# A layer's mixers written as tasks: waits that sleep, marks for order, wider paces

## The chip, the cores and the metric

The kernel runs on one core of one Trainium2 chip. The metric is the device time of one execution in microseconds; the time before is 1107.42 us, the median of three runs from 1107.02 to 1109.54 us. Profiles come from one further execution each. In the profile PE is TensorE (PEld its weight loads), DVE is VectorE, ACT is ScalarE, POOL is GpSimd and SP is SyncE, which issues most transfers.

## The reference

One decoder layer for 256 tokens of width 2048, in float32. Two mixers read one normalised input through one projection, their outputs go through one output projection, and a SwiGLU feed-forward part follows:

```
n = rms_norm(x, attn_norm_g);  proj = n @ w_in          # 2048 -> 5672 columns
g_qkv = silu(causal_short_conv(g_qkv, conv_w))          # q, k, v of the GLA mixer
gla   = gated linear attention (4 heads) of q, k, v, gate(g_lr), rms_norm, * silu(g_out)
nsa   = softmax attention (8 heads, 2 key heads) over compressed, selected and window keys,
        the three summed with sigmoid gates; keys and queries rms-normed
h     = x + concat(gla, nsa) @ w_out
out   = h + (silu(m @ w_gate) * (m @ w_up)) @ w_down    # m = rms_norm(h), d_ff = 5632
```

With 256 tokens all blocks are selected and the window holds all tokens, so the selected and the window branch are two full causal attentions with keys of their own. The compressed branch has 15 keys, each made by a small network from 32 tokens.

## The kernel before, in words

**Arithmetic.** Each large product is made of three matmuls of float32r parts: `hi` of the tokens with `hi` and `lo` of the weights, and `lo` with `hi`. A weight chunk of 512 rows and 512 columns is loaded on SP's queue into `raw` (3 buffers, `load`, L126), then split: ACT copies `hi` (L137), DVE subtracts to `lo` (L138; 4 buffers of 2 rows of tiles each). `chunk` (L273) makes its 24 matmuls (L283) and yields 2 units after each one; where a projection has two column parts, after each pair. A projection (`proj`, L291) is 4 chunks, 192 units; its end `evac` reads the PSUM banks.

**Mains and side tasks.** The order of the work is that of Python generators. `drive(mains, pace)` (L98) runs projections and, for every `pace` units, calls `side()` once (L83). `side` advances one step of a task: the first of the list `urgent`, or, when that is empty, the first of `later`. A task that has to wait for a result of another engine does so by empty yields, each of which uses one call: `for _ in range(8): yield`. `background` holds row sums for the feed-forward part (`sum_rows`, L1068: two loads, four adds on DVE at L1079, two stores on POOL's queue at L1083), one step for every `rate[0]` units. `drain` (L93) runs what is left of a list without any main beside it. The call order ranks the instructions. From it the framework lists each engine's instructions by when it reckons them ready, so that a later call's instruction can stand ahead of an earlier one's: in the profile Exp of the decay (L545) comes before Silu of conv (L502), which is called earlier. Each engine then takes its list in order.

**The tasks.** The stages run in this order: a first projection (low-rank gate and half of the output gate), GO1 (its other half), qq and kk (queries and keys of GLA, pace 1.5), v0 and v1 (its values, pace 2), KC, KS, KW and NQ0 (compressed, selected and window keys with their values, half of NSA's queries, pace 2.5), NQ1 (the other half, pace 2.5), then the first half of w_out (L973, 8 chunks, 384 units, pace 2), the drains of both lists, and the second half of w_out.

- `conv` (L481, urgent; for qq, kk, v0, v1): scaled tokens from ACT (L478), 8 empty calls, then for each of two pairs two calls of transposes (L210), four taps (ACT L490, DVE L492) and `dst`. For values `to_v` (L507) applies Silu (L510, L511), waits 10 calls and transposes again in two.
- `gla_mix` (L647, later): `gla_decay` (L529) has seven levels, each with Exp on ACT (L545, L547), GAP calls, products on DVE and GAP calls again (GAP0 8 for the first pair of heads, GAP1 4 for the second); `gla_scores` (L570) has ten matmuls (L584) for each of four heads; `gla_out` (L602) reads the values and appends `gla_turn` (L628, urgent, 20 empty calls and 2 of transposes).
- `turn_kc` (8 empty calls and 4), `key_turn` (L725, 15 empty calls, 1 of transposes; four of them), `turn_q` (L848, 18 empty calls and 4; two of them), all urgent.
- `compress` (L751, later): for keys and for values, loads of four weight tiles on POOL's queue (L760), 9 calls, 16 small matmuls (L779), again 9 calls and 16 matmuls, then 6 calls, a transpose and Silu (L794 for keys, L798 for values), 9 calls and a matmul (L803 or L819).
- `nsa_mix` (L950, later): for four tiles, `nsa_scores` (L859, 16 calls: L873 to L876) and `nsa_out` (L908, 15 calls for the first half of the tokens and 25 for the second: transposes and L946).

The tiles of 128 partitions and 1024 elements named `g` come in the large from one ring, `g4`, of 24 buffers: the normalised tokens, keys, values, the compression's weights and the row sums share it.

Of the kernel before, what the change touches and what calls it, by code (L numbers as in the profile page):

```python
# [17 lines left out]
NT = S // P  # L18
# [19 lines left out]
def kernel(  # L38
# [42 lines left out]
    urgent, later, background = [], [], []  # L81

    def side():  # L83

        for queue in (urgent, later):
            while queue:
                try:
                    next(queue[0])
                    return
                except StopIteration:  # L90
                    queue.pop(0)

# [121 lines left out]


    cols = kp.tile([P, 164], F32, name="cols")
    pc = bank()
# [7 lines left out]
    def cols_rest():  # L225
        for _ in range(8):
            yield
        nc.gpsimd.memset(w2b, 0.0)
        with behind(last["dma"]):
            small_loads()  # L230
        for _ in range(20):
            yield
        pc = bank()
        transpose(pc[:, 0:P], rows2)
        transpose(pc[:, P:P + 20], rows[:20, :], 20)
        nc.vector.tensor_copy(cols[:, 36:164], pc[:, 0:P])
        nc.vector.tensor_copy(cols[:, 16:36], pc[:, P:P + 20])
        TS(kgain, gains[:, 1:4], gains[:, 0:1], None, ALU.mult)


# [240 lines left out]
    def conv(u, ct, dst):  # L481

        for _ in range(8):
            yield
        for pair in range(2):
            ps = yield from turn_pair(u, pair)
            y = g2([2, S])
            for c in range(2):
                ch = ct + 2 * pair + c
                act(y[:, c, :], ps[:, c, :], AF.Copy, scale=cw[:, 3, ch:ch + 1])  # L490
                for i in range(1, 4):
                    STT(y[:, c, i:], ps[:, c, :S - i], cw[:, 3 - i, ch:ch + 1], y[:, c, i:], ALU.mult, ALU.add)  # L492
            yield from dst(pair, y)
# [6 lines left out]
    def to_qk(near, far):  # L500
        def f(pair, y):
            act(near[:, pair, 0 if near is kk else 1], y[:, :, 0:P], AF.Silu)  # L502
            act(far[:, pair, 0 if far is qq else 1], y[:, :, S - 1:P - 1:-1], AF.Silu)
            yield
        return f

    def to_v(b):  # L507
        def f(pair, y):
            v = g2([2, S])
            act(v[:, :, 0:P], y[:, :, 0:P], AF.Silu)  # L510
            act(v[:, :, P:], y[:, :, S - 1:P - 1:-1], AF.Silu)  # L511
            c0 = (4 * b + 2 * pair) * P
            for _ in range(10):
                yield
            p = bank()
            for t in range(NT):
                for c in range(2):
                    transpose(p[:, t * S + c * P:t * S + (c + 1) * P], v[:, c, t * P:(t + 1) * P])
                yield
            for t in range(NT):  # L520
                nc.scalar.copy(v_sb[t][:, c0:c0 + 2 * P], p[:, t * S:(t + 1) * S])
            v_ready.add(2 * b + pair)
        return f

    m_h, m_l = {}, {}
    v_ready = set()
    GAP0, GAP1 = 8, 4

# [99 lines left out]
    def gla_turn(h, y):  # L628
        for _ in range(20):
            yield  # L630
        if h % 2 == 0:
            m_h[h // 2], m_l[h // 2] = g4([4, S], F32R), g4([4, S], F32R)
        p = bank()
        for j in range(2):
            for t in range(NT):
                transpose(p[:, j * S + t * P:j * S + (t + 1) * P], y[:, t, j * P:(j + 1) * P])
            yield
        put_mix(h // 2, slice(2 * (h % 2), 2 * (h % 2) + 2), slice(0, S), p.rearrange("p (j s) -> p j s", j=2))

    def in_parts(hi, lo, ps):  # L640
# [6 lines left out]
    def gla_mix():  # L647
        res = [{} for _ in range(4)]
        yield from gla_decay(0, GAP0)
        for _ in range(6):  # L650
# [27 lines left out]
    def turn_kc(u):  # L678
        for _ in range(8):
            yield  # L680
        st["uT"] = g4([2, 2, S])
# [43 lines left out]
    def key_turn(br, t, kk):  # L725
        for _ in range(15):
            yield
        p = bank()
# [5 lines left out]
        act(kh, pv, AF.Copy, scale=g)  # L734
        STT(kl, pv, g, f32(kh), ALU.mult, ALU.subtract)

    kcm = cp.tile([P, 2 * NCMP], F32, name="kcm")
# [13 lines left out]
    def compress():  # L751
# [13 lines left out]
        for w in range(2):  # L765
# [20 lines left out]
            nc.vector.tensor_copy(hs, ph[:, :P])  # L786
            for _ in range(6):
                yield
# [6 lines left out]
            else:  # L795
                hid3 = g2([2, P])
                nc.gpsimd.memset(hid3, 0.0)
                act(groups(hid3), thrice(hid[:, :N2].rearrange("p (h n) -> p h n", h=2)), AF.Silu)  # L798
            for _ in range(9):
                yield  # L800
# [47 lines left out]
    def turn_q(kv, q):  # L848
        for _ in range(18):
            yield  # L850
        qf, qh, ql = g4([4, S]), g4([4, S], F32R), g4([4, S], F32R)
# [98 lines left out]
    def nsa_mix():  # L950
# [3 lines left out]
        def ready(u):  # L954
            while u[0] not in nq:
                yield
# [15 lines left out]

    def w_out_half(half):  # L973
        for n in range(4):
            banks = [bank() for _ in range(NT)]
# [299 lines left out]
    def down_last():  # L1275
# [68 lines left out]
        for t, bk in enumerate((banks[4], at[1])):  # L1344
# [11 lines left out]
    drive([proj(1024, ev_conv(8, to_v(0))), proj(1536, ev_conv(12, to_v(1)))], 2)  # L1356
    rate[0] = 18
    drive([proj(C_KC, ev_kc), proj(C_KS, ev_kv(0)),
           proj(C_KW, ev_kv(1), ((0, 256), (256, 280))), proj(C_NQ, ev_nq(0))], 2.5)
    later.append(nsa_mix())  # L1360
    drive([proj(C_NQ + 512, ev_nq(1))], 2.5)
    rate[0] = 14
    drive([w_out_half(0)], 2)
    drain(urgent)
    drain(later)
# [44 lines left out]
```

## Time and profile before

| | us |
|---|---|
| median of 3 runs | 1107.42 |
| lowest, highest | 1107.02, 1109.54 |
| the profiled execution | 1108.26 |
| its span, first to last instruction | 1106.5 |
| PE busy | 1096.7 |
| DVE busy | 992.7 |
| ACT busy | 751.5 |
| POOL busy | 71.7 |

The span is 1.76 us less than the profiled execution's own time; what lies around it is in every run. The first matmul of kk is at 80.79 us, that of KC at 157.09, that of w_out's first half at 291.44 and that of its second half at 369.46; the feed-forward part begins at 416.91 us. In a row of the waits the columns are the sum, the number and the longest; in the timeline, start, length, engine, line, operation, written tile and read tiles, shape, count, and in brackets the idle time before and what ended it.

### The profile page before, as it was taken

Reading aid. Unit: us, or ns where it says so; the run is one execution under the profiler, and the core shown is the slowest. Engines: PE = TensorE matmul, PEld = TensorE weight load, DVE = VectorE, ACT = ScalarE, POOL = GpSimd, SP = SyncE. Lnnn points to the kernel's source line nnn. Section 1 sums busy time; section 2 is a strip of 40 time slices with the busy share of each in tenths; the row PEclk is TensorE's granted clock in tenths of the full one; section 3 lists DMA queues with packets and bytes.
Section 4 is the critical chain, followed back from the end, with each engine's and each line's share of the span. In section 5 each row is a group of like instructions: output and inputs, shape, how many; then the busy total and the mean of one; then the engine's idle time right before and its main releaser. Section 6 shows DMA issues by size and latency. Waiting matters only on the chain.

```text
span 1106.5 us, 14596 instructions
## 1 busy us (share of the span) xinstructions
PE 1096.7 (99%) x5290; PEld 900.4 (81%) x5290; DVE 992.7 (90%) x1277; ACT 751.5 (68%) x1017; POOL 71.7 (6%) x134
## 2 busy tenths in 40 slices
PE   9999999999999999999999999999999999999998
PEld 8888788897777787888888788888888888888886
DVE  6678887879689788997999999999999999999997
ACT  6646867554566596667586776768586866768684
POOL 4110000123200000000000000000000000000000
PEclk9999999999999999999999999999999999999999
DMA  7999677579765646785565657566665657577763
GB/s 271 340 332 346 210 256 243 196 274 375 282 239 192 236 154 218 242 307 200 192 219 202 217 185 256 195 234 215 216 227 201 214 198 252 182 252 234 237 229 114
DMA packets 124850, 259.61 MB, mean 235 GB/s; under 512 B 6709, under 2 KB 8793, under 8 KB 124778
## 3 DMA queue, kind: packets, MB, share of 16 engines
q1 hardware_dynamic: 113514, 219.86, 58.1%
q0 software_dynamic: 10368, 37.75, 9.2%
q10 hardware_dynamic: 896, 1.07, 0.3%
q8 instruction: 41, 0.67, 0.3%
q14 instruction: 31, 0.25, 0.1%
HBM read 239.78 MB, written 18.87 MB: 234 GB/s over the span
## 4 chain that ended last, share of the span: by engine, by line
PE 88%; DVE 5%; DMA 3%; ACT 3%; issue 1%; POOL 0%; ACTq 0%; DVEq 0%
PE bank L283 44%; PE bank L1147 36%; PE bank L210 3%; DMA raw<-in_w_in_dram 2%; PE bank L1288 2%; DVE ftwo L642 2%; DVE lo L138 1%; PE bank L584 1%; PE bank L946 1%; PE bank L873 1%; ACT hi L137 1%; DMA fraw<-in_w_down_dram 1%; ACT ftwo L641 0%; PE bank L779 0%; DVE g L1178 0%
## 5 line engine op out<-in xcount | busy, mean ns | idle before, releaser
L1147 PE MATMUL bank<-ftwo,g 128*128 128x512 f32 x1848 | 431.6, 392 | 0.2 <-ACT ftwo L641 0.2
L1147 PEld LDWEIGHTS bank<-ftwo,g 128*128 128x128 f32 x1848 | 342.4, 188 | 76.6 <-DVE ftwo L642 3.3
L283 PE MATMUL bank<-hi,g 128*128 128x512 f32 (+1 forms) x1088 | 321.5, 375 | 0.3 <-ACT hi L137 0.2
L642 DVE TENSOR_TENSOR ftwo<-fraw,ftwo 128x1536 fp32r<-128x1536 f32 (+1 forms) x130 | 257.9, 1984 | 8.8 <-ACT ftwo L641 7.5
L641 ACT ACTIVATE ftwo<-fraw 128x1536 fp32r<-128x1536 f32 (+1 forms) x130 | 216.9, 1670 | 32.9 <-DMA fraw<-in_w_up_dram 23.2
L283 PE MATMUL bank<-ftwo,g 128*128 128x512 f32 x960 | 221.4, 391 | 0.4 <-ACT bank L1259 0.4
L283 PEld LDWEIGHTS bank<-hi,g 128*128 128x128 f32 x1088 | 192.4, 188 | 31.7 <-issue 0.8
L283 PEld LDWEIGHTS bank<-ftwo,g 128*128 128x128 f32 x960 | 179.2, 188 | 39.9 <-ACT bank L1259 2.6
L137 ACT ACTIVATE hi<-raw 128x1024 fp32r<-128x1024 f32 (+3 forms) x124 | 130.6, 1057 | 95.8 <-PE bank L283 73.2
L283 PE MATMUL bank<-lo,g 128*128 128x512 f32 (+3 forms) x544 | 193.6, 375 | 0.9 <-DVE lo L138 0.6
L138 DVE TENSOR_TENSOR lo<-raw,hi 128x1024 fp32r<-128x1024 f32 (+3 forms) x124 | 150.0, 1216 | 34.3 <-ACT hi L137 33.6
L641 ACT ACTIVATE ftwo<-g 128x1024 fp32r<-128x1024 f32 x74 | 78.2, 1057 | 69.4 <-DVE g L1178 41.1
L283 PEld LDWEIGHTS bank<-lo,g 128*128 128x128 f32 x544 | 98.4, 188 | 16.1 <-DVE lo L138 1.0
L642 DVE TENSOR_TENSOR ftwo<-g,ftwo 128x1024 fp32r<-128x1024 f32 x74 | 90.3, 1220 | 10.5 <-ACT ftwo L641 10.5
L642 DVE TENSOR_TENSOR ftwo<-fsum,ftwo 128x1024 fp32r<-128x1024 f32 x74 | 90.2, 1219 | 0.0
L641 ACT ACTIVATE ftwo<-fsum 128x1024 fp32r<-128x1024 f32 x74 | 77.5, 1048 | 6.4 <-DVE fsum L1180 5.1
L1271 ACT COPY g<-bank 128x512 f32<-128x512 f32 x80 | 45.9, 589 | 39.4 <-PE bank L283 37.6
L1178 DVE TENSOR_TENSOR g<-fraw 128x1024 f32<-128x1024 f32 x56 | 67.5, 1219 | 0.0
L1259 ACT COPY bank<-g 128x512 f32<-128x512 f32 x80 | 45.2, 593 | 14.3 <-DVE f L1208 13.0
L641 ACT ACTIVATE g<-bank 128x512 fp32r<-128x512 f32 x46 | 27.3, 599 | 33.0 <-PE bank L210 27.4
L210 PE MATMUL bank<-ident,g 128*128 128x128 f32 (+3 forms) x230 | 42.5, 277 | 1.5 <-ACT g L1043 0.7
L1136 POOL DMA_DIRECT2D g<-sums x16 | 8.5, 531 | 511.5 <-DVE ftwo L642 482.8
(247 smaller groups left out, 908.3 us busy)
## 6 DMA issues: line engine op xcount, KB each, us to landing
fraw<-in_w_gate_dram SPq DMA_DIRECT2D x86, 512.0 KB, 4.0
fraw<-in_w_down_dram SPq DMA_DIRECT2D x42, 1024.0 KB, 5.1
raw<-in_w_in_dram SPq DMA_DIRECT2D x36, 1024.0 KB, 6.5
fraw<-in_w_up_dram SPq DMA_DIRECT2D x70, 512.0 KB, 4.8
sums<-g POOLq DMA_DIRECT2D x32, 512.0 KB, 5.0
raw<-in_w_out_dram SPq DMA_DIRECT2D x16, 1024.0 KB, 5.8
g<-in_w_gate_dram SPq DMA_DIRECT2D x16, 512.0 KB, 7.4
g<-in_w_up_dram SPq DMA_DIRECT2D x16, 512.0 KB, 8.1
```

What stands on the lines that cost most here:

```text
L137: act(h[:, i:i + n], r[:, k + i:k + i + n], AF.Copy)
L138: last["d"] = TT(o[:, i:i + n], r[:, k + i:k + i + n], f32(h[:, i:i + n]), ALU.subtract)
L210: return nc.tensor.transpose(o, i, ident[:n, :n])
L283: last["mm"] = mm(bk[t], a[:, k, t * P:(t + 1) * P], m[:, off:off + w], start=(first_ and k == 0 and i == 0), stop=(end and k == 3 and i = ...
L584: mm(p[:, j * P:(j + 1) * P], u, w, start=True, stop=True)
L641: act(hi, ps, AF.Copy)
L642: last["d"] = TT(lo, ps, f32(hi), ALU.subtract)
L1147: mm(banks[q], x, m, start=todo[q] == total[q], stop=todo[q] == 1)
L1178: TT(s1, r[:, 1:3], r[:, 3:4].to_broadcast([P, 2, 512]), ALU.add)
L1259: nc.scalar.copy(banks[qs[n][t]], h_sb[n][:, t, :])
L1271: nc.scalar.copy(h_sb[n][:, t, :], bs[t])
L1288: mm(bk, u, m, start=(first and i == 0), stop=(end and i == 2), skip_group_check=onto)
```

## The change

`side` gets a table of sleeping tasks. A task may yield a number; it is then passed over for so many calls, and the call goes to the next task of `urgent` that is awake, or else to the first of `later`. At each call the numbers of all urgent tasks go down by one. The empty yields of conv, to_v, gla_turn, turn_kc, key_turn and turn_q become such numbers, longer than before. The set `done` holds marks: gla_mix waits for the marks of all four pairs of q and k, nsa_mix for those of the four key_turns, and two assertions stand in conv and in w_out. Two waits of the compression grow from 6 to 10 and from 9 to 14 calls, GAP1 from 4 to 6. The paces grow from 2.5 to 2.8 (KC to NQ0), from 2.5 to 2.7 (NQ1) and from 2 to 2.6 (first half of w_out), and the background rate goes from 18 to 16 units from KC on, until the first half of w_out.

```diff
+    asleep = {}
+
     def side():
 
+        for task in urgent:
+            asleep[task] = max(asleep.get(task, 0) - 1, 0)
         for queue in (urgent, later):
-            while queue:
+            while True:
+                task = next((t for t in (urgent if queue is urgent else later[:1]) if not asleep.get(t)), None)
+                if task is None:
+                    break
                 try:
-                    next(queue[0])
+                    asleep[task] = next(task) or 0
                     return
                 except StopIteration:
-                    queue.pop(0)
+                    queue.remove(task)
...
     def conv(u, ct, dst):
 
-        for _ in range(8):
-            yield
+        assert "cols" in done
+        yield 14
...
             act(far[:, pair, 0 if far is qq else 1], y[:, :, S - 1:P - 1:-1], AF.Silu)
+            done.add((near is kk, pair))
             yield
...
             c0 = (4 * b + 2 * pair) * P
-            for _ in range(10):
-                yield
+            yield 16
             p = bank()
...
-    GAP0, GAP1 = 8, 4
+    GAP0, GAP1 = 8, 6
...
     def gla_turn(h, y):
-        for _ in range(20):
-            yield
+        yield 22
...
     def gla_mix():
         res = [{} for _ in range(4)]
+        while not all((i, pair) in done for i in (False, True) for pair in range(2)):
+            yield
         yield from gla_decay(0, GAP0)
...
     def turn_kc(u):
-        for _ in range(8):
-            yield
+        yield 12
...
     def key_turn(br, t, kk):
-        for _ in range(15):
-            yield
+        yield 18
...
         STT(kl, pv, g, f32(kh), ALU.mult, ALU.subtract)
+        done.add(("key", br, t))
...
             nc.vector.tensor_copy(hs, ph[:, :P])
-            for _ in range(6):
+            for _ in range(10):
                 yield
...
-            for _ in range(9):
+            for _ in range(14):
                 yield
             pk = bank()
...
     def turn_q(kv, q):
-        for _ in range(18):
-            yield
+        yield 20
...
         def ready(u):
-            while u[0] not in nq:
+            while u[0] not in nq or not all(("key", br, t) in done for br in range(2) for t in range(NT)):
                 yield
...
     def w_out_half(half):
+        assert all(("out", h) in done for h in range(4))
...
-    rate[0] = 18
+    rate[0] = 16
     drive([proj(C_KC, ev_kc), proj(C_KS, ev_kv(0)),
-           proj(C_KW, ev_kv(1), ((0, 256), (256, 280))), proj(C_NQ, ev_nq(0))], 2.5)
+           proj(C_KW, ev_kv(1), ((0, 256), (256, 280))), proj(C_NQ, ev_nq(0))], 2.8)
     later.append(nsa_mix())
-    drive([proj(C_NQ + 512, ev_nq(1))], 2.5)
+    drive([proj(C_NQ + 512, ev_nq(1))], 2.7)
     rate[0] = 14
-    drive([w_out_half(0)], 2)
+    drive([w_out_half(0)], 2.6)
```

More of the change, by code (lines that the diff above doesn't have):

```diff
@@ L213, in rsqrt_ @@
         nc.gpsimd.tensor_tensor(o, i, mhalf[:i.shape[0], :i.shape[1]], ALU.pow)
+    done = set()
     cols = kp.tile([P, 164], F32, name="cols")
@@ L238, in cols_rest @@
         TS(kgain, gains[:, 1:4], gains[:, 0:1], None, ALU.mult)
+        done.add("cols")
     def flip(src, q, gcol, hi, lo, pairs=range(2), between=None):
@@ L638, in gla_turn @@
         put_mix(h // 2, slice(2 * (h % 2), 2 * (h % 2) + 2), slice(0, S), p.rearrange("p (j s) -> p j s", j=2))
+        done.add(("out", h))
     def in_parts(hi, lo, ps):
```

## The prediction

> **What bounds the kernel now.** I read the page first (busy shares, slices), then the waits of TensorE in the stretch that the change touches, then the timeline around each of those waits, and last the sums by stage.
>
> ```profile
> span 1106.5 us, 14596 instructions
> PE 1096.7 (99%) x5290; PEld 900.4 (81%) x5290; DVE 992.7 (90%) x1277; ACT 751.5 (68%) x1017; POOL 71.7 (6%) x134
> PEclk9999999999999999999999999999999999999999
> 160.67 10.91 PE bank L283 x48
> ```
>
> TensorE is busy 99% of the span at full clock, so the time is the sum of its instructions and of the places where it stands. The last row, from the chain of waits, gives its pace: 10.91/48 = 0.227 us for a 512-column matmul. The change adds and removes no TensorE instruction; it can only move the time by making TensorE stand less, or more, in the mixers (about 80 to 370 us). The waits of TensorE there (75 to 380 us):
>
> ```profile
> PE bank L803 <- ACT g L794: 1.3, 1, 1.3
> PE bank L283 <- DVE lo L138: 0.6, 1, 0.6
> PE bank L210 <- ACT g L510: 0.4, 1, 0.4
> PE bank L210 <- ACT g L478: 0.2, 1, 0.2
> PE bank L283 <- ACT hi L137: 0.2, 1, 0.2
> ```
>
> That is all: 2.7 us by this view. It counts from the modelled end of a matmul, which overlaps the next, so what a wait costs has to be read from start to start in the timeline:
>
> ```profile
> 82.50 0.33 PE L210 MATMUL bank<-ident,g 128*128 128x128 f32 x1
> 83.08 0.33 PE L210 MATMUL bank<-ident,g 128*128 128x128 f32 x1 [0.24 <-ACT g L478]
> 140.09 0.39 PE L283 MATMUL bank<-hi,g 128*128 128x512 f32 x1
> 140.60 1.09 PE L210 MATMUL bank<-ident,g 128*128 128x128 f32 x8
> 180.33 0.39 PE L283 MATMUL bank<-hi,g 128*128 128x512 f32 x1
> 181.12 0.44 PE L210 MATMUL bank<-ident,g 128*128 128x128 f32 x2 [0.41 <-ACT g L510]
> 273.43 0.27 PE L210 MATMUL bank<-ident,g 128*128 128x128 f32 x1
> 276.06 0.39 PE L283 MATMUL bank<-hi,g 128*128 128x512 f32 x1
> 277.74 0.40 PE L803 MATMUL bank<-cw,g 128*30 128x128 f32 x2 [1.29 <-ACT g L794]
> 17.32 0.87 PE bank L210 x8
> ```
>
> Two transposes in one group start 0.87/8 = 0.109 apart when nothing is late (last row, chain of waits). So L210 at 83.08 is 0.58 - 0.11 = 0.47 late, at 140.60 0.51 - 0.23 = 0.28, at 181.12 0.79 - 0.23 = 0.56, and L803 1.68 - 0.23 = 1.45. In each the matmuls of the projection that come behind needed nothing from the mixer: the mixer's instruction was put ahead of them before its input was there. Sum: **2.76 us**. The fifth place is of another kind:
>
> ```profile
> 119.09 1.28 ACT L547 ACT_TABLE_LOAD   x1
> 120.71 1.05 ACT L137 ACTIVATE hi<-raw 128x1024 fp32r<-128x1024 f32 x1
> 121.19 0.39 PE L283 MATMUL bank<-hi,g 128*128 128x512 f32 x1
> 121.81 0.73 PE L283 MATMUL bank<-hi,g 128*128 128x512 f32 x2 [0.23 <-ACT hi L137]
> 123.12 0.50 PE L283 MATMUL bank<-lo,g 128*128 128x512 f32 x1 [0.58 <-DVE lo L138]
> ```
>
> Here the projection itself waits for its own split weights: 0.62 - 0.23 = 0.39 and 1.31 - 0.46 = 0.85, together 1.24 us, because ACT was behind with the mixer's Silu and Exp and their table loads.
>
> **The change part by part.** One side call is made for every `pace` units, and a matmul of a projection is 2 units.
>
> *Waits made longer.* A task that slept n calls as n empty yields ran at call n+1; `yield n` sleeps through n calls after the first, the same call n+1. In conv that is call 9 against 15, at pace 1.5 (kk): 6 x 0.75 matmuls x 0.227 = 1.02 us later, against 0.47 needed. In to_v, call 11 against 17: at pace 2 in the first value projections 6 x 0.227 = 1.36 us, against 0.28; in KC at paces 2.5 and 2.8, 11 x 1.25 = 13.8 against 17 x 1.4 = 23.8 matmuls, 2.28 us later, against 0.56. Before L803: 10 calls x 1.25 x 0.227 = 2.84 us, which the rows show (273.43 to 276.29, where L803 would have stood without its wait); after, 15 x 1.4 x 0.227 = 4.77 us, against 277.74 - 273.43 = 4.31 that its input took. So all four waits are covered, the last by 0.46 us only: -2.76 us. What is late next there is nothing in the waits' list.
>
> *Sleeping tasks leave their calls to others.* No instruction comes of this, only a denser order. I count the calls per stage. Before, conv of a value projection takes 36 calls (8 + 2 x 14) in which nothing else is called; after, 11. The GLA mixer gets 60 calls in v1 before and 85 after; its second decay costs 57 calls before and 85 after (GAP1 6), and it ends about call 45 of KS's 68 instead of at the start of NQ0. The compression (97 calls before, 115 after) then runs from KS to about call 41 of NQ0. The NSA mixer has 4 x 16 + 2 x (15 + 25) + 2 = 146 calls. Before, w_out's first half had 384/2 = 192 calls: 22 for turn_q, 19 left of the compression, 146: 187, nearly all. The trace agrees:
>
> ```profile
> L946 PE MATMUL bank<-g,g x36: 387/394/502, 324.4 to 368.3; 128*128 128x512 f32 x36
> 369.00 0.40 PE L283 MATMUL bank<-lo,g 128*128 128x512 f32 x1
> ```
>
> After, it gets some 47 calls in NQ1 (71 calls, free from call 25 on) and the other 99 from call 25 of w_out's 147: done at call 124, 23 before the end. So the wider paces leave nothing to the drains behind that stage, and I cost them at nothing. If the sleeping freed no calls, 187 would not fit in 147, and 40 calls would run with no projection beside them.
>
> *Scatter.* Calls that were piled up and ran in one go (the 8 transposes at 140.60 are four calls) now stand apart. What a group apart costs:
>
> ```profile
> 270.46 0.38 PE L210 MATMUL bank<-ident,g 128*128 128x128 f32 x2
> 270.92 0.38 PE L210 MATMUL bank<-ident,g 128*128 128x128 f32 x2
> ```
>
> 0.46 from group to group, for 2 x 0.109 + 0.227 = 0.445 of work: 0.015 each. Between none and thirty more groups: 0 to 0.45 us; I take ten, +0.15: the four calls at 140.60 make three, and there were two value projections and the scores piled up in the same way.
>
> *Marks.* The guards in gla_mix and nsa_mix spend calls that emit nothing (about 20 and 24); no engine waits and nothing is queued behind. The assertions emit nothing. *Rate 18 to 16* in the four projections: 768/16 = 48 background steps for 43, so two of the sixteen row sums move some steps ahead, two loads, four adds on DVE and two stores on POOL's queue each. They lie beside matmuls before and after:
>
> ```profile
> 157.10:181.30 24.20, 23.79 (x111) 19.11 (x110) 20.31 (x37) 14.79 (x24) 1.06 (x2) 1.00 0.60 196
> 212.20:239.50 27.30, 27.30 (x217) 27.01 (x216) 20.46 (x37) 13.86 (x31) 3.01 (x5) 1.00 0.59 200
> 239.50:265.00 25.50, 25.50 (x170) 20.36 (x169) 22.14 (x51) 12.33 (x26) 9.22 (x12) 1.00 1.03 370
> ```
>
> These are KC, KW and NQ0 (length, PE, PEld, DVE, ACT, POOL, clock, DMA share, GB/s). The compression's loads leave NQ0, where the DMA engines are full, for stages at 0.6: nothing, or a small gain. DVE stands at 0.75 to 0.87, so denser calls fit.
>
> *Sum*: -2.76 + 0.15 = -2.6 us. The profiled execution took 1108.26 us, which would become 1105.7; it lies 0.84 above the median of the runs, so against 1107.42 I forecast **1104.8 us**. The 1.24 us at 121.81 I leave in: conv(kk) and the first decay keep their order and distance there (Silu at calls 17 and 20, first Exp at 21; before 11, 14 and 15).
>
> **The rivals.** *The gain is taken back by table loads (or the waits move with the calls).*
>
> ```profile
> L510 ACT ACT_TABLE_LOAD  x2: 1283/1283/1283, 138.8 to 169.8; - x2
> L545 ACT ACT_TABLE_LOAD  x4: 1283/1283/1283, 109.0 to 181.4; - x4
> 108.98 1.28 ACT L545 ACT_TABLE_LOAD   x1
> 110.28 0.44 ACT L545 ACTIVATE g<-g 128x256 f32<-128x256 f32 x1
> ```
>
> Before, the decay's Exp (L545) stays away between the two Silus of a value projection (L510): 2 loads for each projection. After, the sleep of 16 calls between them is given to the decay: up to 4 each, 4 more in all, 5.1 us of ACT. If that makes the split weights late twice as it did at 121.81, 2 x 1.24 = 2.5 us come back: 1107.3. For it: that very place. Against: ACT is busy 14.79 of 24.20 us in KC, and the two other pairs of loads made no split late. The Trainium skill says in "ScalarE: Activation LUTs", section "Table sets: the hidden batching unit", that calls should be batched by table set, and in "What ACT_TABLE_LOAD costs" that a switch takes 1283 ns and a drain of about 1380 ns more. The load agrees to the nanosecond; the drain does not show, since Exp starts at 110.28 after a load at 108.98, and I keep to the trace. By the page, as an estimate, the four switches would be 10.6 us of ACT and, in proportion, 5.2 us would come back: 1110.0. The same result, 1107.4, comes if the waits stay: the order is set by when an instruction is reckoned to be ready, and the calls only rank them.
>
> *Slower: the compression's weights come late.*
>
> ```profile
> L760 POOL DMA_DIRECT2D g<-in_cmp_k_w_dram x4: 886/908/954, 240.8 to 247.2; - x4
> DMA to landing us min/median/max: 7.2/7.7/8.9
> L779 PE MATMUL bank<-g,g x128: 272/273/296, 259.0 to 299.2; 128*30 128x128 f32 x128
> ```
>
> Between the loads' place (L760) and their first use (L779) stand 10 calls, unchanged. Before, the 54 calls of gla_turn and key_turn ahead of them let POOL issue the loads 18.2 us before L779. After, those sleep, and the code stands directly behind the GLA mixer: if the loads go out only at their place, the second is issued after 1.8 us and lands after 9.5, the calls give 10 x 1.4 x 0.227 = 3.2, and TensorE stands 6.3 us: 1111.1. It undoes the gain when the loads lead by under 6.9 us. Against it: the loads need only free buffers of the g4 ring, and four that kh, kl, vh and vl held by then are still free in KS.
>
> *Faster still*: ACT's pile-up at 109 to 120 us falls otherwise and the 1.24 go too: 1103.6.
>
> **How the numbers follow.** A measurement of this kernel tells from no change about 0.2%, 2.2 us: faster means under 1105.2, slower over 1109.6. The forecast has 0.45, with a range of its own from 1104.2 to 1105.5; 0.07 of it lies over 1105.2. Faster still 0.15; taken back or unmoved 0.26; late weights 0.14. So faster 0.38 + 0.15 = 0.53, same 0.07 + 0.26 = 0.33, slower 0.14. From 1103.0 (faster still, without the 0.15, and the 0.4 by which the lowest run lies under the median) to 1108.5 (unmoved, with a last wait of 1 us) the range leaves out the late weights and a little below.
>
> **What would show it.** Right: the waits of TensorE no longer list L803 behind L794 nor L210 behind L510 or L478; the last L946 lies some 7 us before the end of w_out's first half; the first L779 has no wait. Wrong: new rows of L283 behind L137 or L138 with more table loads between the rows of L510 (rival one); L779 waiting for L760's DMA (rival two); a drained tail, matmuls of L946 with none of L283 between them, after that half.

## The result and the profile after

The changed kernel takes 1116.75 us, the median of four runs from 1115.58 to 1117.83; the kernel before took 1108.48 beside it (1107.02 to 1109.73). The ratio is 1.0075, with a 95% interval from 1.0056 to 1.0094: some 8 us slower, where 2.6 us less were forecast, and outside the range given. The profiled execution is the longest of the four, 1117.83 us, with a span of 1116.1 against 1106.5: 9.6 us more, which are accounted for here. In the places that matter the lines of the changed kernel stand seven to ten further down (L283 is now L292, L210 L217, L510 L520, L545 L554, L584 L593, L642 L651, L803 L813, L946 L955, L1079 L1089, L1106 L1116, L1147 L1157).

The page after, span, busy shares and granted clock by slices:

```profile
span 1116.1 us, 14593 instructions
PE 1099.1 (98%) x5290; PEld 903.1 (81%) x5290; DVE 994.0 (89%) x1277; ACT 756.8 (68%) x1021; POOL 71.0 (6%) x134
PEclk9999998999999999999999999999999999999999
```

TensorE and DVE do the same number of instructions. ACT has four more and is busy 5.3 us longer: four table loads of 1.28 us are 5.1. And one slice of the clock, which was 9 throughout, shows 8. The waits of TensorE after, from 75 to 380 us (sum, number, longest):

```profile
PE bank L217 <- ACT g L520: 3.7, 2, 3.5
PE bank L217 <- DVE g L796: 1.4, 1, 1.4
PE bank L789 <- DVE g L784: 1.0, 1, 1.0
PE bank L882 <- DVE g L651: 0.7, 1, 0.7
PE bank L813 <- ACT g L804: 0.5, 1, 0.5
PE bank L950 <- DVE g L939: 0.3, 1, 0.3
```

7.6 us against the 2.7 of before. Both rows of weights that were late before (hi L137, lo L138) are gone, and so is L210 behind L478. L803 behind L794 has shrunk (L813 behind L804). But L210 behind L510, 0.4 us before, is 3.7 now, and four rows are new. The largest place, at the end of KC, with ACT, DVE and TensorE in the order of time (timeline, after):

```profile
168.59 1.28 ACT L520 ACT_TABLE_LOAD   x1 [1.23 <-DVE g L501]
170.63 1.28 ACT L554 ACT_TABLE_LOAD   x1
177.90 0.39 PE L292 MATMUL bank<-hi,g 128*128 128x512 f32 x1
178.91 1.05 ACT L144 ACTIVATE hi<-raw 128x1024 fp32r<-128x1024 f32 x1
179.27 0.48 DVE L501 SCALAR_TENSOR_TENSOR g<-bank,cols,g 128x253 f32<-128x253 f32 x1
179.97 1.28 ACT L520 ACT_TABLE_LOAD   x1
181.26 0.42 ACT L520 ACTIVATE g<-g 128x256 f32<-128x256 f32 x1
181.73 1.11 PE L217 MATMUL bank<-ident,g 128*128 128x128 f32 x4 [3.45 <-ACT g L520]
184.21 0.77 PE L292 MATMUL bank<-hi,g 128*128 128x512 f32 x1
```

At 177.90 the last matmul of KC starts. The next in TensorE's list are transposes of the last value pair; they start 3.83 us later instead of 0.23, a stand of 3.6 us. They wait for Silu (L520), Silu for its table load, and that load for the last tap of conv (L501). The first matmul of KS, at 184.21, comes behind the transposes; by the order of the splits, those that it reads ended at 174.50 (hi) and 175.85 (lo), over 8 us before. Nothing of it was late but its place in the list. The same Silu before:

```profile
180.66 0.41 ACT L510 ACTIVATE g<-g 128x256 f32<-128x256 f32 x1
```

So against the kernel before, Silu starts 0.60 us later, and TensorE is through with KC 2.43 us earlier (last matmul at 177.90 for 180.33): together 3.03 us more to wait.

What comes behind the stand shows in the windows (length, PE, PEld, DVE, ACT, POOL, clock, DMA share, GB/s):

```profile
181.50:188.00 6.50, 6.27 (x25) 5.72 (x26) 4.45 (x13) 4.85 (x12) 0.00 (x0) 0.55 0.97 344
188.00:194.00 6.00, 6.00 (x34) 5.08 (x34) 3.56 (x11) 2.43 (x7) 0.72 (x1) 1.00 0.22 83
```

The granted clock is 0.55 of full speed in the 6.5 us behind the stand; in the timeline the instruction behind a matmul of 512 columns starts 0.43 us after it there (184.78 to 185.21), against 0.23 elsewhere. The trace's clock record has one stretch at half, 6.83 us long, from 180.54 on. The Trainium skill says in "TensorE: Matmul & The Clock Gate", section "What's actually happening", that the clock falls to half after about 3.4 us of idleness and comes back after as much work. The trace agrees in part: the clock is halved in such a stand, but already 2.25 us behind the modelled end of the last matmul (178.29), and for 6.83 us. It could have been foreseen as soon as a stand of that size was thought possible, which it wasn't.

Last, the feed-forward part. Its first matmuls with `ftwo`, before and after (first and last start):

```profile
L1147 PE MATMUL bank<-ftwo,g x1848: 387/389/504, 429.0 to 1058.7; 128*128 128x512 f32 x185
```

```profile
L1157 PE MATMUL bank<-ftwo,g x1848: 387/389/505, 435.4 to 1068.4; 128*128 128x512 f32 x185
```

435.4 - 429.0 = 6.4 us are lost ahead of it, and (1068.4 - 435.4) - (1058.7 - 429.0) = 3.3 us inside it, where the change touches no line. The waits of SP's queue, and the places where SP and TensorE pay (after):

```profile
SPq L1116 <- DVE g L651: 21.1, 1, 21.1
```

```profile
431.56 0.37 SPq L1116 DMA_DIRECT2D fraw<-in_w_gate_dram  x1
450.23 1.67 PE L1157 MATMUL bank<-ftwo,g 128*128 128x512 f32 x6 [0.91 <-DVE ftwo L651]
453.12 1.20 PE L1157 MATMUL bank<-ftwo,g 128*128 128x512 f32 x4 [1.22 <-DVE ftwo L651]
```

In the trace of before:

```profile
419.01 0.37 SPq L1106 DMA_DIRECT2D fraw<-in_w_gate_dram  x1
```

The second weight chunk of the part is issued at 431.56; before, it was at 419.01. SP waits 21.1 us for a DVE instruction of the turn of `h`, a mixer-pool tile whose memory the weights' buffer takes over. Twice TensorE then has no weights, from start to start 1.7 and 1.5 us. Read in this way, the stands sum up as follows (us, profiled executions):

| place | before | after | forecast |
|---|---|---|---|
| the four waits that were to go (end of KC 0.56, then 3.61; L803 1.45, then 0.62; 0.47 and 0.28, then none) | 2.76 | 4.23 | 0 |
| late split weights at 121.81 and 123.12 | 1.24 | 0 | 1.24 |
| new: L217 at 149.59 (0.37), L789 (1.13), L217 behind L796 (1.59), L950 (0.45), L882 (0.90) | 0 | 4.44 | 0 |
| what is left of the 6.4 us ahead of the feed-forward part: halved clock, scatter | | 1.7 | 0.15 |
| feed-forward part | | 3.3 | 0 |

Changes: +1.5 - 1.2 + 4.4 + 1.7 + 3.3 = 9.7, for the 9.6 of the spans.

### The profile page after: what moved, and what is told of

The parts are those of the page before. It is cut to its first block, busy times and chain, and to the rows that moved or that the text cites. A ratio compares the mean times of both kernels' runs of the same rounds, so it can differ in the third digit from the quotient of the medians.

```text
span 1116.1 us, 14593 instructions
## 1 busy us (share of the span) xinstructions
PE 1099.1 (98%) x5290; PEld 903.1 (81%) x5290; DVE 994.0 (89%) x1277; ACT 756.8 (68%) x1021; POOL 71.0 (6%) x134
## 4 chain that ended last, share of the span: by engine, by line
PE 79%; DVE 7%; issue 7%; DMA 3%; ACT 2%; POOL 1%; ACTq 0%; SPq 0%; POOLq 0%; DVEq 0%
PE bank L292 42%; PE bank L1157 30%; DVE ftwo L651 4%; PE bank L217 2%; PE bank L1298 2%; DMA g<-in_w_up_dram 1%; DMA fraw<-in_w_up_dram 1%; DVE g L1188 1%; PE bank L955 1%; PE bank L593 1%; DMA sums<-g 1%; ACT ftwo L650 1%; DMA fraw<-in_w_down_dram 1%; PE bank L882 1%; DMA raw<-in_w_in_dram 1%
## 5 line engine op out<-in xcount | busy, mean ns | idle before, releaser
L1157 PE MATMUL bank<-ftwo,g 128*128 128x512 f32 x1848 | 432.6, 393 | 2.6 <-DVE ftwo L651 2.1
L1157 PEld LDWEIGHTS bank<-ftwo,g 128*128 128x128 f32 x1848 | 342.3, 188 | 80.0 <-DVE ftwo L651 6.3
L292 PE MATMUL bank<-hi,g 128*128 128x512 f32 (+1 forms) x1088 | 323.8, 376 | 0.8 <-ACT hi L332 0.8
L651 DVE TENSOR_TENSOR ftwo<-fraw,ftwo 128x1536 fp32r<-128x1536 f32 (+1 forms) x130 | 258.0, 1986 | 11.7 <-ACT ftwo L650 10.4
L292 PE MATMUL bank<-ftwo,g 128*128 128x512 f32 x960 | 221.4, 391 | 0.3 <-ACT bank L1269 0.3
L292 PEld LDWEIGHTS bank<-hi,g 128*128 128x128 f32 x1088 | 191.8, 189 | 30.1 <-ACT hi L332 1.2
L292 PEld LDWEIGHTS bank<-ftwo,g 128*128 128x128 f32 x960 | 179.2, 188 | 39.8 <-ACT bank L1269 2.4
L144 ACT ACTIVATE hi<-raw 128x1024 fp32r<-128x1024 f32 (+3 forms) x124 | 130.6, 1057 | 99.0 <-PE bank L292 77.9
L292 PE MATMUL bank<-lo,g 128*128 128x512 f32 (+3 forms) x544 | 193.2, 374 | 0.1
L145 DVE TENSOR_TENSOR lo<-raw,hi 128x1024 fp32r<-128x1024 f32 (+3 forms) x124 | 149.9, 1219 | 35.9 <-ACT hi L144 35.4
L292 PEld LDWEIGHTS bank<-lo,g 128*128 128x128 f32 x544 | 98.7, 189 | 15.1 <-DVE lo L145 0.4
L651 DVE TENSOR_TENSOR ftwo<-g,ftwo 128x1024 fp32r<-128x1024 f32 x74 | 90.3, 1221 | 10.6 <-ACT ftwo L650 10.5
L651 DVE TENSOR_TENSOR ftwo<-fsum,ftwo 128x1024 fp32r<-128x1024 f32 x74 | 90.3, 1220 | 0.0
L217 PE MATMUL bank<-ident,g 128*128 128x128 f32 (+3 forms) x230 | 42.5, 278 | 5.8 <-ACT g L520 3.7
L217 PEld LDWEIGHTS bank<-ident,g 128*128 128x128 f32 (+3 forms) x230 | 31.1, 144 | 17.6 <-ACT g L520 4.5
```

What stands on the lines that cost most here:

```text
L144: act(h[:, i:i + n], r[:, k + i:k + i + n], AF.Copy)
L145: last["d"] = TT(o[:, i:i + n], r[:, k + i:k + i + n], f32(h[:, i:i + n]), ALU.subtract)
L217: return nc.tensor.transpose(o, i, ident[:n, :n])
L292: last["mm"] = mm(bk[t], a[:, k, t * P:(t + 1) * P], m[:, off:off + w], start=(first_ and k == 0 and i == 0), stop=(end and k == 3 and i = ...
L651: last["d"] = TT(lo, ps, f32(hi), ALU.subtract)
L1157: mm(banks[q], x, m, start=todo[q] == total[q], stop=todo[q] == 1)
```

## The experiments

Times are medians in us, ratios are to the kernel before on the same chip, with 95% intervals.

**Which part of the change does it.** First, only the mechanism: sleep and marks, with all numbers, paces and the rate of before.

```diff
-        yield 14
+        yield 8
...
-            yield 16
+            yield 10
...
-    GAP0, GAP1 = 8, 6
+    GAP0, GAP1 = 8, 4
...
-    drive([w_out_half(0)], 2.6)
+    drive([w_out_half(0)], 2)
...
```

> Sleeping tasks and marks alone: all numbers of calls, GAP1, paces and the rate are those of before. Theory A: the calls that sleeping tasks leave bring the scores and the last value transposes ahead of KS's first matmul here too, so TensorE stands 2 to 4 us there: 1112 to 1117 us. Theory B (the numbers do it): 1107 to 1110 us.

Measured: 1128.65, ratio 1.0187 [1.0172, 1.0203]. The largest waits of TensorE, 75 to 380 us:

```profile
PE bank L217 <- ACT g L520: 8.4, 2, 5.0
PE bank L217 <- DVE g L732: 2.2, 3, 0.9
PE bank L616 <- DVE g L588: 2.0, 1, 2.0
```

The sleep by itself costs some 21 us, and the value transposes behind Silu are the largest part: stands of 3.6 and 5.2 us, with the clock halved behind both. The longer numbers, the paces and the rate of the change together win 12 of the 21 back. So the change is a loss with a partial repair. Next, the paces and the rate alone, put back to those of before:

```diff
-    rate[0] = 16
+    rate[0] = 18
...
-           proj(C_KW, ev_kv(1), ((0, 256), (256, 280))), proj(C_NQ, ev_nq(0))], 2.8)
+           proj(C_KW, ev_kv(1), ((0, 256), (256, 280))), proj(C_NQ, ev_nq(0))], 2.5)
```

> The changed kernel with the paces (2.5, 2.5, 2) and the background rate (18) of before; sleeping, waits and marks stay. Theory A: in TensorE's list the last value transposes still stand ahead of KS's first matmul, so it stands 2 to 4 us there: 1113 to 1117 us. Theory B: 1108 to 1110 us.

Measured: 1116.96, ratio 1.0082 [1.0066, 1.0098], with the same stand of 3.61 us at 181.74. In sum paces and rate do nothing to the time, so the repair lies in the longer numbers; the forecast cost paces and rate at nothing and was right there.

**The end of KC.** One number, the sleep ahead of the value transposes:

```diff
-            yield 16
+            yield 24
```

> The changed kernel, but to_v sleeps 24 calls instead of 16. Theory A: the last transposes then stand behind several of KS's matmuls in TensorE's list, their Silu is done by then, the 3.6 us and the half clock go: 1110 us. Theory B: nothing changes in the paces, 1115 to 1117 us.

Measured: 1109.67, ratio 1.0016 [1.0006, 1.0026], 7.1 us less than the kernel after. Waits of TensorE, 75 to 380 us:

```profile
PE bank L217 <- DVE g L796: 1.5, 1, 1.5
PE bank L292 <- DVE lo L145: 1.4, 1, 1.4
PE bank L789 <- DVE g L784: 1.0, 1, 1.0
...
```

L217 behind L520 is gone, no stretch of the clock is halved, and the wait of 21.1 us on SP's queue is gone with it. The other rows stay within 0.1 us, and one of split weights (L292 behind L145, 1.6 us from start to start) is new. That the 1110 expected came so near is in part luck: of the 8.2 us between the two spans 3.4 are the feed-forward part's, which now lasts 629.6 us for 633.0, and only 4.8 lie ahead of it. The same place from another side, the old empty calls for this one wait:

```diff
-            yield 16
+            for _ in range(10):
+                yield
```

> The changed kernel, but to_v waits its 10 calls awake, by empty yields, as before the change. Theory A (one wait): the loss of the mixers sits where KC ends, where TensorE stands 3.6 us before the transposes of the last value pair and then runs some 7 us at half clock, together about 6.5 us; with to_v awake no scores are called between the Silus and these transposes come one by one beside KS's matmuls: 1110 us, no granted clock under 1 inside the span. Theory B (paces): the loss comes from the wider paces and the background rate, which this kernel keeps: 1115 to 1117 us.

Measured: 1118.78, ratio 1.0097 [1.0082, 1.0112]: slower still, where 1110 was expected. At the end of KC it did what was expected, the stand is 0.57 us as before. But two new ones of 3.2 and 3.0 us stand at 255.57 and 259.86, where transposes wait for the scaling of keys on DVE (here L733), and one of 2.2 us at 225.30 behind L634:

```profile
PE bank L217 <- DVE g L733: 5.7, 2, 2.9
```

```profile
DVE g L1090 <- DMA g<-in_w_up_dram: 8.1, 2, 7.4
```

The second row is DVE's: its list holds a row sum's add (L1090) whose load had not landed, 7.4 us long, and the keys are behind it. The place was mended, and in the other order of calls a wait of another kind stands in the path.

Why is Silu late at the end of KC? In the next kernel the value projections' Silu is a Copy, which needs no table.

```diff
-            act(v[:, :, 0:P], y[:, :, 0:P], AF.Silu)
-            act(v[:, :, P:], y[:, :, S - 1:P - 1:-1], AF.Silu)
+            act(v[:, :, 0:P], y[:, :, 0:P], AF.Copy)
+            act(v[:, :, P:], y[:, :, S - 1:P - 1:-1], AF.Copy)
```

> The changed kernel with Copy instead of Silu on the values, so that the decay's Exp needs no table load behind them (the output lacks that Silu). In TensorE's list the last value transposes still stand ahead of KS's first matmul. If the table load of 1.28 us is a third of the wait of 3.6 us, 2.3 us are left, too short for the half clock: 1111 to 1113 us. If the wait is the four taps on VectorE alone, it stays 3 us or more: 1115 to 1117 us.

Measured: 1111.72, ratio 1.0039 [1.0025, 1.0053]. The same place in the timeline:

```profile
177.67 0.41 ACT L520 ACTIVATE g<-g 128x256 f32<-128x256 f32 x1
177.97 0.41 ACT L521 ACTIVATE g<-g 128x256 f32<-128x256 f32 x1
178.13 0.44 PE L217 MATMUL bank<-ident,g 128*128 128x128 f32 x2 [0.41 <-ACT g L520]
```

With the transposes still listed behind KC's last matmul the stand is 0.57 us, 3.04 less, and the clock keeps full speed. The time is within what was expected, but by another sum: one load was to go and 2.3 us to stay. From 120 to 200 us ACT loads no table here, eight in the kernel after, four in the kernel before. Three of the eight lie in KC ahead of the last Silu, 3 x 1.28 = 3.84 us on a chain that goes from ACT's scaled tokens to DVE's taps and back to Silu. So the stand needs both: a Silu made late by the loads (e6), and transposes listed ahead of KS (e2, where they come later).

Are DVE's adds (0.68 us each, between the taps) part of that lateness? A kernel without row sums in KC:

```diff
-    rate[0] = 16
-    drive([proj(C_KC, ev_kc), proj(C_KS, ev_kv(0)),
+    rate[0] = 0
+    drive([proj(C_KC, ev_kc)], 2.8)
+    rate[0] = 12
+    drive([proj(C_KS, ev_kv(0)),
```

> The kernel after, but with no row sums at all during KC (rate 0 there, 12 units from KS to NQ0, so that no step is lost): DVE's taps of conv have none of the sums' adds (0.68 us each) between them. On TensorE the transposes of the last value pair still stand ahead of KS's first matmul. If the eight table loads alone make Silu late, the stand of 3.6 us at the end of KC stays over 3 us and the clock is halved behind it again: 1115 to 1117 us. If the adds have a share in it, the stand falls to 2.2 us or less and full clock is kept: 1111 to 1113.

Measured: 1123.66, ratio 1.0139 [1.012, 1.0157]: neither case. The stand at the end of KC grew to 6.1 us, and one of 5.6 us came at 238.93. ACT and DVE ahead of it:

```profile
169.18 1.06 ACT L144 ACTIVATE hi<-raw 128x1024 fp32r<-128x1024 f32 x1 [1.93 <-DMA raw<-in_w_in_dram]
...
179.95 0.68 DVE L1089 TENSOR_TENSOR g<-g,g 128x512 f32<-128x512 f32 x1
180.54 0.48 DVE L501 SCALAR_TENSOR_TENSOR g<-bank,cols,g 128x254 f32<-128x254 f32 x1
180.94 0.68 DVE L1089 TENSOR_TENSOR g<-g,g 128x512 f32<-128x512 f32 x1
181.54 0.48 DVE L501 SCALAR_TENSOR_TENSOR g<-bank,cols,g 128x253 f32<-128x253 f32 x1
```

The adds called in KS were listed among the taps of KC all the same, so the edit did not take them away; and ACT's list had a split of weights, waiting 1.93 us for its DMA, ahead of the first Silu. What this run shows is how far ahead the list reaches. The adds' share stays open.

**The feed-forward part.** The last tiles of the turn of `h` get memory that the weights' buffers don't take over:

```diff
-            v = g2([2, S])
+            v = (g4 if n == 3 else g2)([2, S])
```

> The kernel after, with one edit in the turn of h: its last tiles v (n of 3) come from the ring g4 instead of g2, whose memory the feed-forward part's raw buffers take over. If the feed-forward part is 3.1 us longer than before because its second weight loads wait for those late tiles (SP's wait of 21.1 us on L651), that wait goes, the loads issue at about 410 us instead of 431.6, and the time is 1113.0 to 1114.2 us. If the loads are late for another reason, or the 3 us come from another place: 1116 to 1117.5.

Measured: 1112.47, ratio 1.0043 [1.0028, 1.0058]. SP's queue, then the first and last matmul, then the window of the stand:

```profile
412.77 0.37 SPq L1116 DMA_DIRECT2D fraw<-in_w_gate_dram  x1
```

```profile
L1157 PE MATMUL bank<-ftwo,g x1848: 387/389/504, 433.4 to 1062.7; 128*128 128x512 f32 x185
```

```profile
181.50:188.00 6.50, 5.67 (x35) 4.61 (x36) 4.48 (x14) 4.59 (x11) 0.00 (x0) 1.00 0.96 333
```

The time is half a microsecond under the range expected. The load goes out 18.8 us earlier, the wait of 21.1 us is gone, and the part lasts 629.3 us from first to last of these matmuls, against 633.0 after and 629.7 before. So the 3.3 us of the feed-forward part come from that shared memory. The last row brings something unasked: the stand at the end of KC is still 3.6 us, but the clock is 1.00 behind it, and 35 matmuls fit where there were 25. The same stand halves the clock in one execution and not in another: of the four executions of the kernel after, one has a mean clock of 1.000, two 0.998 and one 0.997.

**What is left once the end of KC is mended.** Wider waits in the compression, on top of the sleep of 24 (9 to 14, 10 to 18, 14 to 18 calls):

```diff
-            for _ in range(10):
+            for _ in range(18):
```

> The changed kernel with to_v's sleep of 24 calls and the compression's three waits at 14, 18 and 18 calls instead of 9, 10 and 14. Theory A (each loss is a mixer's instruction that stands in TensorE's list before its input is there): the waits that the run with 24 calls still showed in the compression (1.6 us before the transposes behind L796, 1.1 before L789, 0.8 before L813) go, 1106 to 1107 us. Rival: they move to the next instruction of the chain, 1109 to 1111 us.

Measured: 1116.57, ratio 1.0083 [1.0068, 1.0099]. The three stands at L789, L796 and L813 are gone and one of 7.0 us is there instead (timeline, DVE and TensorE):

```profile
229.14 0.69 DVE L1089 TENSOR_TENSOR g<-g 128x512 f32<-128x512 f32 x1 [5.36 <-DMA g<-in_w_up_dram]
231.44 0.61 DVE L732 TENSOR_SCALAR g<-bank,sm 128x128 f32<-128x128 f32 x2
231.84 0.73 PE L217 MATMUL bank<-ident,g 128*128 128x128 f32 x2 [6.81 <-DVE g L732]
```

Again an add that waits for its load in DVE's list, a key's scaling behind it, and transposes behind that in TensorE's list. The kernel before with the longer waits as empty calls (paces 2.1, 2.1 and 1.65 to give as many more calls) has no sleep at all:

```diff
-        for _ in range(8):
+        for _ in range(14):
             yield
...
-    drive([w_out_half(0)], 2)
+    drive([w_out_half(0)], 1.65)
```

> The kernel before with all the longer waits of the change as empty yields (nobody sleeps) and paces of 2.1, 2.1 and 1.65 so that the calls suffice. If the sleeping is the cause, since it gives the calls of a wait to work that keeps ACT and VectorE from the waiting task: 1106 to 1109 us. If it is the place in TensorE's list alone (here too the last value transposes and scores stand ahead of KS's first matmul): a stand of 2 to 4 us at KC's end and 1111 to 1115 us.

Measured: 1111.12, ratio 1.0029 [1.0017, 1.0042]. L803 behind L794 is gone, and this stands in its place:

```profile
PE bank L210 <- DVE g L837: 4.2, 2, 3.8
```

```profile
DVE g L1079 <- DMA g<-in_w_up_dram: 10.0, 3, 8.0
```

Longer waits without sleep lose as well, by DVE's wait of 8.0 us for a row load ahead of L837; behind that stand, 3.9 us from start to start, the clock is halved for 3.41 us. The smallest edit of that kind, in the kernel before, only the two waits of the compression and a pace of 1.85 in w_out:

```diff
-            for _ in range(6):
+            for _ in range(10):
```

> The kernel before with only the compression's two longer waits (10 and 14 calls), and a pace of 1.85 for w_out's first half so that the calls suffice. The prediction's term of 1.45 us for L803 alone: 1106.0 us and no wait before L803. Rival (the wait moves): 1107.5 us, with another wait of 1 us or more in the compression.

Measured: 1108.16, ratio 1.0009 [0.9999, 1.0019]. L803's 1.45 us went as the forecast had it, and 1.67 us appeared at 324.75, where L941 waits for DVE's L930. A covered wait is not yet a gain.

**Row sums later.** If adds in DVE's list cause these stands, they must come later, or in another stage. First two steps later in the same stages (a rate of 14 and 11 to make room), in four kernels: e7's (e9), the sleep of 24 (e10), the empty calls in to_v (e11) and the kernel before (e12).

```diff
-        for _ in range(3):
+        for _ in range(5):
             yield True
```

> The kernel with the longer waits awake, and the row sums' adds two steps later behind their loads (5 instead of 3), background rates 14, 11 and 11. Theory D: its stand of 3.9 us and the half clock came from VectorE, which stood 8.0 us in front of such an add for its load, with the keys' and queries' work behind it in its list. Then they go: 1105 to 1106.5 us. Rival (the transposes come too early by their own calls): 1110 us or more.

> The changed kernel with to_v's sleep of 24 calls and the same later adds. VectorE stood 3.1 us in front of an add there too, but after the transposes had already waited 1.6 us. Theory D therefore gives little: 1108.5 to 1110 us. If VectorE's waits are behind all of what is left: 1106 us.

> The changed kernel with to_v awake and the same later adds. Theory D: the two stands of 3 us before the keys' transposes and their half clock (VectorE stood 7.4 us for a row load with the keys' scaling behind it) go: 1108 to 1111 us. Rival (sleeping key_turns come too early by themselves): 1116 us or more.

> Control: the kernel before with the later adds alone. VectorE stood 2.5 us for a row load there and no TensorE wait stood behind it: 1107 to 1108 us.

Measured: 1112.94 (1.0052 [1.0035, 1.0069]); 1110.35 (1.0020 [1.0010, 1.0030]); 1114.79 (1.0061 [1.0046, 1.0076]); 1111.78 (1.0037 [1.0024, 1.0050]). None came in where the adds' waits alone would have put it. Only the third won, 4.0 us from 1118.78: its stands at L733 are gone, others of 2.2 and 2.5 us came. In the first DVE still waits 7.0 us for a row load, and TensorE stands 4.5 us. In the second DVE waits for no row load from 75 to 380 us, yet the stand behind L796 grew from 1.6 to 2.8. The kernel before lost 4.2 us (1107.58 beside it), as L803's stand grew to 3.9. So two steps more mend one kernel of four; the denser rate changes all the rest with it.

Then most row sums out of KC to NQ1 and into w_out (one step for 32 units, then one for 8):

```diff
-    rate[0] = 16
+    rate[0] = 32
...
-    rate[0] = 14
+    rate[0] = 8
     drive([w_out_half(0)], 2.6)
```

> The kernel before with all waits longer and paces 2.1, 2.1 and 1.65 (e7), and with few row sums from KC to NQ1 (one step for 32 units) and many beside the first half of w_out (one for 8). If DVE's wait of 8 us for a row load in NQ1 is what is left, the stand of 3.9 us at 293.7 and its halved clock go: 1106 to 1108 us. If the order of TensorE's list is at fault whatever DVE does, a stand appears elsewhere: 1110 us or more.

> The kernel after with a sleep of 24 calls in to_v (e2), and with few row sums from KC to NQ1 (one step for 32 units) and many beside the first half of w_out (one for 8). If the row sums cause the stands that were left (1.1, 1.6 and 0.8 us at 211 to 232 us): 1107.5 to 1109. If these come from the calls alone: 1109.7 or more.

Measured: 1111.57, ratio 1.0034 [1.0021, 1.0047], where e7 took 1111.12; and 1106.44, ratio 0.9985 [0.9975, 0.9995], where the sleep of 24 took 1109.67. In the first the stand at L837 and DVE's wait did go, but in w_out, where many adds now are, a split of weights came late:

```profile
PE bank L283 <- DVE lo L138: 2.4, 1, 2.4
PE bank L210 <- ACT g L882: 1.6, 1, 1.6
```

In the second DVE waits 0.4 us for row loads (4.2 us in three places with the sleep of 24), and these are all the waits of TensorE from 75 to 380 us:

```profile
PE bank L217 <- DVE g L796: 2.1, 1, 2.1
PE bank L882 <- DVE g L651: 0.2, 1, 0.2
```

It is the first version under the kernel before, by 0.15%, less than the 0.2% that the prediction called a difference. To see whether that is one lucky order of calls, one number of it is changed, and as a control for e16 the tile's ring alone:

```diff
-            yield 24
+            yield 28
```

> The kernel with the late row sums (e15) and a sleep of 28 calls instead of 24 in to_v. If the late row sums free these stages of stands whatever the calls, the time stays within 1.5 us of e15: 1105 to 1108. If e15 is one lucky order of many, a stand of over 2 us appears that e15 doesn't have: 1109 or more.

> The kernel with the sleep of 24 calls and the late row sums (e15), with the same edit in the turn of h. The second weight loads of the feed-forward part did not wait there (issued at 407.5 us), so it should change nothing in that part: 1105.8 to 1107.0 us. If the ring's other users are moved by it and a stand appears: over 1108.

Measured: 1106.23, ratio 0.9991 [0.9981, 1.0000], with a longest stand of 1.5 us; and 1106.91, ratio 0.9987 [0.9977, 0.9996]. Both stay where e15 is, so it isn't one order of calls alone that made it. Waits of TensorE with the sleep of 28:

```profile
PE bank L217 <- DVE g L796: 1.3, 1, 1.3
PE bank L789 <- DVE g L784: 0.5, 1, 0.5
PE bank L882 <- DVE g L651: 0.2, 1, 0.2
```

## Why the prediction was wrong

**The four waits.** The step that failed is the one on value projections: "call 11 against 17 ... 2.28 us later, against 0.56", and behind it "What is late next there is nothing in the waits' list". The covers were worked out as if the inputs stayed where they were. For conv, for L803 and for the first value projections that was near enough (0.47 gone, 1.45 to 0.62, 0.28 gone). At the end of KC the transposes were still listed right behind KC's last matmul, which came 2.43 us earlier. Silu came 0.60 us later, though the scaled tokens of its conv start 3.12 us earlier (153.25 for 156.37): the sleep that was to make room for Silu let the decay's Exp in between the Silus, and the loads made Silu 3.6 us later than it is without them (181.26 against 177.67 in e6). A term of -0.56 became +3.05, a stand of 3.61 us where none was to be left.

**Table loads, rival one.** Its count was right to the load, eight for four. Its place was wrong: it had the split weights late again at 2.5 us, but these had 5.3 us in hand even without the stand (184.78 - 175.85 - 3.61), and no L292 waits for L144 or L145 in KC. The reader of the late Silu itself was not thought of. Without the loads the kernel is 5.0 us faster (1116.75 against 1111.72), twice the rival's price: 3.04 us of the stand and, with it, stands of 0.37 (at 149.59) and 0.62 us (L813). The 1.0 us left may be the halved clock or scatter. The drain that the Trainium skill's "ScalarE: Activation LUTs" adds in its section "What ACT_TABLE_LOAD costs" does not show after the change either: the load at 179.97 is followed by Silu at 181.26.

**What is late next.** It was said to be nothing; it was 4.4 us in five places. The forecast's own sentence, that "a later call's instruction can stand ahead of an earlier one's", was used against rival one and not against itself. With 85 calls in place of 60 in v1, and the compression ahead by as many, DVE meets row sums, taps and keys at once where it had them in turn; that is an argument, no run counts it. E1, e5 and e7 show the new stands of 3 to 7 us that other orders bring: in each DVE's list has an add that waits 5.4 to 8.0 us for its load, with what TensorE needs behind it. For the five places of the changed kernel itself the cause stays open. In e10, where DVE waits for no row load, and in e15, where most adds are elsewhere, L789, L950 and most of L882 are gone, but L796 is longer (2.8 and 2.3 us for 1.6). E8 and e12 show that a few calls more or less move such stands.

**The feed-forward part.** Not in the forecast at all. The step was left out: the 3.3 us stood at nothing without a reason. A mixer's tile that is read last decides when the part's second weights load, and which tile has that memory changes with the order of the calls. E16 shows it: the part is 3.7 us shorter. The wait on SP's queue isn't itself the price: in e7 it is 20.1 us, and the part lasts 630.3 us, 0.6 more than before.

**The 1.24 us at 121.81.** They were left in, and they went. That was the condition of "faster still", and it was met without the outcome; why they went, no run shows.

**What held.** The calls were counted right: the last L955 starts at 368.33 and the second half of w_out at about 375.8, 7.5 us before its end, against "some 7 us". Paces and rate were worth nothing (e3). Rival two didn't happen: L789 waits 1.0 us for DVE's L784, not for its weights; only with the old numbers (e4) does it wait for them, 0.9 us.

**Open.** What in the framework places that tile in the buffer of the weights; how much of Silu's lateness is DVE's adds; what makes the five new stands; why the stand at L520 is 5.2 us in e4; and what late row sums bring to the kernel before without the sleep, which no run has: what e15 owes to the sleep is not shown.

## What to carry to other kernels

Where a planner lists each engine's instructions and the engines take them in order, a longer wait is worked out against the input's new time, with everything on its engines that the freed calls let in, and not against the lateness of the old trace. When a side task's transposes can be listed ahead of a main matmul that is ready, a stand of 3 us can cost more than 3: ask for the halved clock behind it. An instruction that waits for a DMA can hold up all that is listed behind it on an engine that feeds the critical one (5.4 to 8.0 us in e1, e5 and e7). Moving the row sums to a stage with room brought 3.2 us in one kernel (e2 to e15) and nothing in another (e7 to e14), so such a move has to be measured with the order that it makes.

## What the runs showed of the hardware

The halving of TensorE's clock came in stretches of 3.41 or 6.83 us in all traces. Behind the same stand of 3.61 us at the end of KC it was 6.83 us in the kernel after, 3.41 in e3 and nothing in e16. Stands of 2.2 us (e1), 2.3 (e15) and 3.9 us (e7) were followed by 3.41 us at half, one of 7.0 us (e5) by 6.83; one of 2.4 us (e4) and one of 2.5 us (e11) by none, and none came behind a stand of 1.8 us or less. So in this program it has to be reckoned with from some 2.2 us on, and its length isn't fixed by the stand.

Its price isn't fixed either. In the kernel after, 25 instructions of TensorE lie in the window of 6.5 us at 0.55, where 35 lie at full clock in e16, but e16's feed-forward part started only 435.4 - 433.4 = 2.0 us earlier, as it then had other stands (0.4 and 1.0 us at 185.99 and 187.41, the second behind DVE). The execution of the kernel after with a mean clock of 1.000 took 1116.61 us, no less than the two at 0.998 (1115.58 and 1116.89). In e15 and e18, with seven executions at 0.999 or more and three at 0.998 each, these three took 1.4 and 2.1 us longer in the mean.
